# A hybrid decoder trunk on one core: one more feed-forward block by seven products, and ordinary work in pieces

## The chip, the cores and the metric

The kernel runs on one core of one Trainium2 chip. The metric is the device time of one execution in microseconds. A core has TensorE (PE, with its weight loads shown as PEld), VectorE (DVE), ScalarE (ACT), GpSimd (POOL) and SyncE (SP), each with an instruction queue of its own that is worked off in order. Matmuls write banks of PSUM; VectorE and ScalarE read them.

## The reference

Two layers work on 256 tokens of width 2048, all in float32:

```python
for l in range(DEPTH):                          # 2
    h = rms_norm(x, norm1_g[l])
    z = h @ w_in[l]                             # 2048 x 3584
    out_a = chunked_sgu(gelu(z[..., :2048]), ...)
    out_b = swa_sink_attention(...)             # window 128, 16 heads
    mixed = concat(rms_norm(out_a), rms_norm(out_b))
    x = x + mixed @ w_out[l]                    # 2048 x 2048
    h2 = rms_norm(x, norm2_g[l])
    x = x + (silu(h2 @ w_gate[l]) * (h2 @ w_up[l])) @ w_down[l]   # 2048 x 5632, back 5632 x 2048
```

The change lies in the last line, the feed-forward part.

## The kernel before, in words

Tokens lie in two tiles of 128. Weights arrive in chunks of 128 x 1024 numbers (512 KB): `raw_load` (L86) takes one of seven `raw` buffers in turn and issues the load on SP's queue. `split2` (L93) makes two parts of the chunk that together carry more of the float32 than one: ScalarE casts it to `wh` (L99), VectorE subtracts that from the chunk to give `wl` (L100). There are five buffers of each. `mm3` (L137) then multiplies activations and weights with three matmuls, high by high, high by low, low by high (L138 to L140), each 512 columns wide. The activations were transposed by TensorE beforehand and split in the same way.

The feed-forward width of 5632 is cut into 11 blocks of 512 columns. A block is done in one of two ways.

- *Ordinary* (`gate_up`, `even`, `unit`): 8 chunks of `w_gate` and 8 of `w_up`, each chunk with 12 matmuls over both token tiles, into two banks named `dacc`. ScalarE applies SiLU to the gate sums (L679), VectorE multiplies in the up sums (L683).
- *By seven products* (`seven`): gate and up for two token tiles form a 2 x 2 product of matrices, which a scheme of the Strassen kind does with seven products where the plain way has eight. Each chunk here (`s_unit`) serves one product with 6 matmuls. The activations' sums are made once per layer (`ext`). Per fourth of the inner width VectorE forms three sums of weight chunks (L613, L614, L619), and GpSimd's queue adds one more chunk into the tile `t2` with an accumulating load (L621). In the first phase five products go to five banks `m`; VectorE then combines them with five adds (L632 to L638). In the second phase the last two products go to two further banks `n`, which two adds (L651) bring in; SiLU and two multiplications (L652, L654) finish the block.

`S_BLOCKS` (L43) names the blocks that go by seven products: 3 to 10. Blocks 0 to 2 are ordinary. When a block is finished, `act_later` sets two calls of `act_T` (L573), two or three chunks later, each of which transposes 256 columns through one PSUM bank of the pool `pm` and splits them into a tile `aT` (L577, L578). The pool has ACTS = 6 of these.

`down` multiplies finished blocks by `w_down`. For each group of one or two blocks and each of four column ranges it runs 2 or 4 chunks of 12 matmuls into `dacc`, and VectorE adds the result to the residual `xres` (L704). Such work is ordinary as well: 12 matmuls for each split.

The two kinds of work are woven together when the program is recorded. A seven-product chunk gives VectorE more to do than TensorE, an ordinary chunk less. `debt` counts VectorE's assumed cost (VEC, VEC_P) less LOAD times TensorE's (MM); while it is positive, the loop takes chunks from `std_stream`:

```python
        other = std_stream()
        debt[0] = 0.0
        for _ in s_stream():
            while debt[0] > 0.0 and next(other, False):
                pass
```

`std_stream` follows `STD_ORDER` (L44) strictly: a `down` group whose transposed blocks are not there yet yields False, and nothing ordinary is taken in its place. What is left when the seven-product blocks are done runs at the end of the layer (the tail). On top of this the tile framework orders each engine's instructions when it records the program.

Of the kernel before, what the change touches and what calls it, by code (L numbers as in the profile page):

```python
# [21 lines left out]
P = 128  # L22
# [3 lines left out]
L = 2  # L26
# [13 lines left out]
NI = 3584 // NB  # L40
NFF = DFF // NB
ND = D // NB
S_BLOCKS = (3, 4, 5, 6, 7, 8, 9, 10)  # L43
STD_ORDER = (  # L44
    ("gu", 0), ("down", (0, 3)), ("gu", 1), ("down", (1, 4)), ("down", (5, 6)), ("gu", 2),
    ("down", (2, 7)), ("down", (8, 9)), ("down", (10,)),
)
ACTS = 6
VEC = 1.14
VEC_P = 0.6  # L50
MM = 0.227
LOAD = 0.91
RL = 512
WARM = 12

# [12 lines left out]
def trunk(ctx, tc, x, xt, w_in, w_out, w_gate, w_up, w_down, sgu_w, sgu_g, consts,  # L68
# [39 lines left out]

    def vec(n, cost=VEC):
        debt[0] += n * cost  # L110
# [7 lines left out]
    def later(delay, fn):  # L118
        pending.append((clock[0] + delay, next(serial), fn))
# [14 lines left out]
        pool, tag = ((pm, "sm"), (pd, "dacc"), (pa, "acc"), (pd, "dacc"))[next(turns) % 4]  # L134
        return pool.tile(shape, F32, tag=tag, name=name)

    def mm3(acc, ah, al, wh, wl, first, last):  # L137
        nc.tensor.matmul(acc, ah, wh, start=first, stop=False)  # L138
        nc.tensor.matmul(acc, ah, wl, start=False, stop=False)  # L139
        nc.tensor.matmul(acc, al, wh, start=False, stop=last)  # L140

    def unit(src, acts, acc, first, last):
        raw = raw_load(src, 2 if clock[0] < 4 else 1)
# [131 lines left out]
    for lay in range(L):  # L275
# [297 lines left out]
        def act_T(b, c, sg, pairs_f=pairs_f):  # L573
            ps = pm.tile([P, 2, SEQ], F32, tag="sm", name="ps_f")
            transpose_pair([sg[t][:, 2 * c * P : (2 * c + 2) * P] for t in range(NTOK)], ps)
            pair = pair_tile("aT")
            nc.scalar.copy(pair[:, 0], ps)  # L577
            nc.vector.tensor_tensor(pair[:, 1], ps, f(pair[:, 0]), ALU.subtract)  # L578
            vec(1, VEC_P)
            pe(2)  # L580
            pairs_f.setdefault(b, []).append(pair)

        def act_later(b, sg, act_T=act_T):
            for c in range(2):
                later(2 + c, lambda c=c: act_T(b, c, sg))

        def seven(b, lay=lay, pairs2=pairs2, ext2=ext2, act_later=act_later):
            bank = [pa.tile([P, NB], F32, tag="acc", name=f"m{i}") for i in range(5)]

            def s_unit(raw, m, i, op, first, last):  # L590
                wh, wl = split2(raw)
                for j in range(2):
                    ah, al = (op(2 * i + j, h) for h in range(2))
                    mm3(bank[m], ah, al, wh[:, j, :], wl[:, j, :], first and j == 0, last and j == 1)
                pe(6)
                tick(0.5)

            def a_op(k, t):
                return lambda p, h: pairs2[p][:, h, k, t * P : (t + 1) * P]

            def e_op(n):
                return lambda p, h: ext2[p][:, h, n, :]

            kept = []
            for i in range(4):
                b11 = raw_load(w_gate[lay, b, i, 0])
                b12 = raw_load(w_up[lay, b, i, 0])
                b22 = raw_load(w_up[lay, b, i, 1])
                t2 = ap.tile([P, 2, NB], F32, tag="spt", name="t2", bufs=4)
                first, last = i == 0, i == 3  # L610
                s_unit(b11, 0, i, a_op(0, 0), first, last)
                yield
                nc.vector.tensor_tensor(b11, b11, b12, ALU.add)  # L613
                nc.vector.tensor_tensor(t2, b11, b22, ALU.add)  # L614
                s_unit(b11, 1, i, e_op(1), first, last)
                vec(1)
                vec(1)
                yield
                nc.vector.tensor_tensor(b12, b12, b22, ALU.add)  # L619
                s_unit(t2, 3, i, e_op(2), first, last)  # L620
                nc.gpsimd.dma_start(t2, w_gate[lay, b, i, 1], accum_op=ALU.add)  # L621
                vec(1)
                yield
                s_unit(b12, 2, i, e_op(0), first, last)
                yield
                s_unit(b22, 4, i, e_op(3), first, last)
                yield
                kept.append(t2)
            m1 = zp.tile([P, NB], F32, tag="z", name="m1")
            nc.scalar.copy(m1, bank[0])  # L630
            u1 = zp.tile([P, NB], F32, tag="z", name="u1")
            nc.vector.tensor_tensor(u1, bank[3], m1, ALU.add)  # L632
            c22 = zp.tile([P, NB], F32, tag="z", name="c22")
            c21 = zp.tile([P, NB], F32, tag="z", name="c21")
            nc.vector.tensor_tensor(c21, bank[2], u1, ALU.add)
            nc.vector.tensor_tensor(c22, bank[1], c21, ALU.add)
            nc.vector.tensor_tensor(u1, bank[1], u1, ALU.add)
            nc.vector.tensor_tensor(u1, bank[4], u1, ALU.add)  # L638
            vec(5, VEC_P)
            yield  # L640
            bank = [pa.tile([P, NB], F32, tag="acc", name=f"n{i}") for i in range(2)]
            for i in range(4):
                b21 = raw_load(w_gate[lay, b, i, 1])
                first, last = i == 0, i == 3
                s_unit(b21, 0, i, a_op(1, 0), first, last)
                yield
                s_unit(kept[i], 1, i, a_op(1, 1), first, last)
                yield
            sg = [m1, c21]
            for t, m in ((0, m1), (1, c21)):  # L650
                nc.vector.tensor_tensor(m, bank[t], m, ALU.add)  # L651
                nc.scalar.activation(m, m, AF.Silu, scale=rstd2[t])  # L652
            for t, c in ((0, u1), (1, c22)):
                nc.vector.scalar_tensor_tensor(sg[t], c, nrstd2[t], sg[t], ALU.mult, ALU.mult)  # L654
            vec(4, VEC_P)
            act_later(b, sg)
            yield

        seven_done = [False]

        def s_stream(seven=seven):
            for b in S_BLOCKS:
                yield from seven(b)
# [7 lines left out]
                    yield True  # L671
            return acc

        def gate_up(b, even=even, act_later=act_later):
            acc = yield from even(b, w_gate)
            sg = []
            for t in range(NTOK):
                s = zp.tile([P, NB], F32, tag="z", name="sg")
                nc.scalar.activation(s, acc[t], AF.Silu, scale=rstd2[t])  # L679
                sg.append(s)  # L680
            acc = yield from even(b, w_up)
            for t in range(NTOK):
                nc.vector.scalar_tensor_tensor(  # L683
                    sg[t], acc[t], rstd2[t], sg[t], ALU.mult, ALU.mult
                )
            vec(NTOK, VEC_P)
            act_later(b, sg)

        def down(blocks, final, lay=lay, pairs_f=pairs_f, norm_block=norm_block, ss1=ss1, pairs1=pairs1):
            for n in range(ND):  # L690
                while any(len(pairs_f.get(b, [])) < 2 for b in blocks):
                    yield False
                acc = new_acc() if seven_done[0] else new_acc(pd, "dacc")
                for k, b in enumerate(blocks):
                    for c in range(2):
                        pair = pairs_f[b][c]
                        unit(
                            w_down[lay, b, n, c], [(pair, 0), (pair, 1)], acc,
                            k == 0 and c == 0, k == len(blocks) - 1 and c == 1,
                        )  # L700
                        yield True
                for t in range(NTOK):
                    xs = xres[:, t, n * NB : (n + 1) * NB]
                    nc.vector.tensor_tensor(xs, acc[t], xs, ALU.add)  # L704
                    vec(1, VEC_P)
                    if final and lay == L - 1:
                        nc.sync.dma_start(out[t * P : (t + 1) * P, n * NB : (n + 1) * NB], xs)
                if final and lay < L - 1:
                    norm_block(n, ss1, pairs1, lay + 1, C_G1)

        def std_stream(gate_up=gate_up, down=down):
            for k, (kind, what) in enumerate(STD_ORDER):
                if kind == "gu":
                    yield from gate_up(what)
                else:
                    yield from down(what, k == len(STD_ORDER) - 1)

        other = std_stream()
        debt[0] = 0.0
        for _ in s_stream():  # L720
            while debt[0] > 0.0 and next(other, False):
                pass
        seven_done[0] = True
        for went in other:
# [90 lines left out]
```

## Time and profile before

| | |
|---|---|
| three runs | 1959.99, 1961.52, 1965.34 us; median 1961.52 us |
| profiled execution | 1963.79 us, span 1962.1 us, granted clock 1.000 |
| PE busy, wide matmuls | 1947.1 us (99%); 8942 matmul instructions |
| VectorE busy | 1660.7 us (85%) |
| ScalarE busy | 1131.1 us (58%) |
| GpSimd busy | 120.3 us (6%) |
| HBM read | 416.47 MB, 214 GB/s over the span with the writes |
| feed-forward part, layer 0 and layer 1 | first `m` matmul at 288.3 and 1264.4 us |

The span runs from the first to the last instruction; the device time has 1.7 us more around it. Busy shares are means over stages: in the attention part VectorE is busy for 31 to 42 of 50 us, in the feed-forward part for 43 to 49. A matmul's row has a modelled end and overlaps the next row, so TensorE's pace is read from the starts.

### The profile page before, as it was taken

How to read it: one execution, taken by the hardware profiler on the slowest of the kernel's cores; microseconds unless marked ns; L12 is line 12 of the kernel's file. 1: busy time of each engine (PE TensorE's matmuls, PEld its weight loads, DVE VectorE, ACT ScalarE, POOL GpSimd, SP SyncE). 2: the span in 40 equal slices, each digit the busy share in tenths (PEclk: the TensorE clock that was granted, in tenths of full speed). 3: DMA queues.
4: the chain of work that ended last, by engine and by line, in shares of the span. 5: the costliest groups of instructions: out<-in, count | busy, mean ns of one | idle time of the engine just before them, and what ended most of it. 6: DMA issues, size and time to landing. Idle time of an engine off the chain costs nothing.

```text
span 1962.1 us, 24613 instructions
## 1 busy us (share of the span) xinstructions
PE 1947.1 (99%) x8942; PEld 1596.4 (81%) x8942; DVE 1660.7 (85%) x1883; ACT 1131.1 (58%) x1429; POOL 120.3 (6%) x129
## 2 busy tenths in 40 slices
PE   9999999999999999999999999999999999999999
PEld 7788888878878888888888888888888788888887
DVE  6776689989989899999667866899899898999984
ACT  7465566655655556656455565666556565565562
POOL 1210000000000000000002100000000000000000
PEclk9999999999999999999999999999999999999999
DMA  8854558677686776867655455676776767767773
GB/s 319 270 167 154 189 165 245 202 235 215 219 257 207 230 239 198 255 220 244 195 187 192 158 162 183 185 232 195 234 234 222 242 213 226 238 216 253 217 244 108
DMA packets 118554, 420.22 MB, mean 214 GB/s; under 512 B 13040, under 2 KB 15216, under 8 KB 118432
## 3 DMA queue, kind: packets, MB, share of 16 engines
q1 hardware_dynamic: 106928, 377.57, 55.7%
q0 software_dynamic: 11360, 41.00, 11.8%
q8 instruction: 70, 1.15, 0.2%
q14 instruction: 52, 0.43, 0.1%
q10 hardware_dynamic: 144, 0.08, 0.0%
HBM read 416.47 MB, written 4.23 MB: 214 GB/s over the span
## 4 chain that ended last, share of the span: by engine, by line
PE 88%; DVE 7%; DMA 3%; issue 2%; ACT 1%; POOL 0%; SPq 0%; ACTq 0%; DVEq 0%
PE dacc L138 10%; PE dacc L139 10%; PE dacc L140 10%; PE acc L138 9%; PE acc L140 9%; PE acc L139 9%; PE m L140 6%; PE m L139 6%; PE m L138 6%; DVE wl L100 3%; PE n L140 3%; PE n L139 3%; PE n L138 3%; PE ps_v L399 1%; DMA raw<-in_w_in_dram 1%
## 5 line engine op out<-in xcount | busy, mean ns | idle before, releaser
L99 ACT CAST wh<-raw 128x1024 fp32r<-128x1024 f32 (+1 forms) x770 | 794.1, 1049 | 657.4 <-PE acc L140 162.9
L100 DVE TENSOR_TENSOR wl<-raw,wh 128x1024 fp32r<-128x1024 f32 (+1 forms) x770 | 920.2, 1218 | 193.3 <-ACT wh L99 184.7
L138 PE MATMUL dacc<-wh,aT 128*128 128x512 f32 x576 | 225.2, 393 | 4.1 <-DVE xres L704 3.6
L139 PE MATMUL dacc<-wl,aT 128*128 128x512 f32 x576 | 225.0, 391 | 0.0
L140 PE MATMUL dacc<-wh,aT 128*128 128x512 f32 x576 | 224.8, 390 | 0.0
L139 PE MATMUL m<-wl,ext 128*128 128x512 f32 x512 | 200.6, 392 | 1.2 <-DVE wl L100 1.1
L138 PE MATMUL m<-wh,ext 128*128 128x512 f32 x512 | 200.1, 391 | 0.4 <-ACT wh L99 0.4
L140 PE MATMUL m<-wh,ext 128*128 128x512 f32 x512 | 199.4, 389 | 0.0
L138 PE MATMUL acc<-wh,hT 128*128 128x512 f32 x448 | 180.3, 404 | 0.2 <-ACT wh L99 0.2
L139 PE MATMUL acc<-wl,hT 128*128 128x512 f32 x448 | 175.4, 391 | 0.8 <-DVE wl L100 0.8
L140 PE MATMUL acc<-wh,hT 128*128 128x512 f32 x448 | 175.3, 391 | 0.0
L99 ACT CAST wh<-t 128x1024 fp32r<-128x1024 f32 x128 | 134.7, 1053 | 49.3 <-PE dacc L140 26.3
L100 DVE TENSOR_TENSOR wl<-t,wh 128x1024 fp32r<-128x1024 f32 x128 | 155.8, 1217 | 8.2 <-ACT wh L99 5.3
L138 PE MATMUL dacc<-wh,hT 128*128 128x512 f32 x384 | 151.1, 394 | 1.4 <-ACT sg L679 1.1
L138 PE MATMUL acc<-wh,aT 128*128 128x512 f32 x384 | 151.3, 394 | 0.0
L140 PE MATMUL acc<-wh,aT 128*128 128x512 f32 x384 | 149.8, 390 | 0.0
L139 PE MATMUL dacc<-wl,hT 128*128 128x512 f32 x384 | 149.7, 390 | 0.0
L140 PE MATMUL dacc<-wh,hT 128*128 128x512 f32 x384 | 149.7, 390 | 0.0
L139 PE MATMUL acc<-wl,aT 128*128 128x512 f32 x384 | 149.7, 390 | 0.0
L621 POOL DMA_DIRECT2D t<-in_w_gate_dram x64 | 54.7, 854 | 1337.8 <-DVE wl L100 769.7
L138 PEld LDWEIGHTS dacc<-wh,aT 128*128 128x128 f32 x576 | 107.7, 188 | 29.5 <-DVE xres L704 6.2
L139 PEld LDWEIGHTS dacc<-wl,aT 128*128 128x128 f32 x576 | 108.2, 188 | 22.9 <-DVE wl L100 0.8
(150 smaller groups left out, 2973.4 us busy)
## 6 DMA issues: line engine op xcount, KB each, us to landing
raw<-in_w_gate_dram SPq DMA_DIRECT2D x176, 512.0 KB, 5.5
raw<-in_w_up_dram SPq DMA_DIRECT2D x176, 512.0 KB, 4.5
raw<-in_w_down_dram SPq DMA_DIRECT2D x176, 512.0 KB, 4.6
raw<-in_w_in_dram SPq DMA_DIRECT2D x108, 512.0 KB, 4.5
raw<-in_w_out_dram SPq DMA_DIRECT2D x64, 512.0 KB, 3.3
t<-in_w_gate_dram POOLq DMA_DIRECT2D x64, 512.0 KB, 7.2
bias<-rdram POOLq DMA_DIRECT2D x8, 512.0 KB, 5.4
raw<-in_w_in_dram SPq DMA_DIRECT2D x8, 256.0 KB, 5.6
```

Source lines behind the costliest of these rows:

```text
L99: nc.scalar.copy(wh[:, j : j + step, :], src)
L100: nc.vector.tensor_tensor(wl[:, j : j + step, :], src, f(wh[:, j : j + step, :]), ALU.subtract)
L138: nc.tensor.matmul(acc, ah, wh, start=first, stop=False)
L139: nc.tensor.matmul(acc, ah, wl, start=False, stop=False)
L140: nc.tensor.matmul(acc, al, wh, start=False, stop=last)
L399: nc.tensor.matmul(pv[:, i, :], pt[:, i * nkb + b, :], zkv[b][:, (NKV + g) * HD : (NKV + g + 1) * HD], start=b == 0, stop=b == nkb - 1,)
L621: nc.gpsimd.dma_start(t2, w_gate[lay, b, i, 1], accum_op=ALU.add)
```

## The change

Block 2 goes by seven products too, nine blocks instead of eight. Ordinary work is cut into pieces: the gate half of a block, its up half, and each column range of a `down` group. At the end of each piece the first piece in `STD_ORDER` whose inputs are there is taken. A finished block's transposes are held (`held`) until a tile `aT` is left for them after what earlier groups still need (`room`, `admit`); after a first phase, ordinary work is taken also while more than HOLD = 2 are held. LOAD goes from 0.91 to 0.95. In `seven` the second phase adds onto bank 0 and bank 2 of the first phase, in which the other results already stand, with no fresh banks, and each sum tile's chunk comes one place later. The combination has four adds, the second phase one, and SiLU reads bank 0 in PSUM.

```diff
-S_BLOCKS = (3, 4, 5, 6, 7, 8, 9, 10)
+S_BLOCKS = (2, 3, 4, 5, 6, 7, 8, 9, 10)
 STD_ORDER = (
-    ("gu", 0), ("down", (0, 3)), ("gu", 1), ("down", (1, 4)), ("down", (5, 6)), ("gu", 2),
-    ("down", (2, 7)), ("down", (8, 9)), ("down", (10,)),
+    ("gu", 0), ("down", (0, 2)), ("down", (3, 4)), ("gu", 1), ("down", (1, 5)), ("down", (6, 7)), ("down", (8, 9)), ("down", (10,)),
 )
 ACTS = 6
+HOLD = 2
-LOAD = 0.91
+LOAD = 0.95
...
+        def room(b, made=made, freed=freed):
+            at = next(i for i, c in enumerate(chunks) if b in c)
+            missing = sum(2 - made.count(x) for c in chunks[:at] for x in c)
+            return len(made) - freed[0] + missing < ACTS
+
+        def admit(act_T=act_T, held=held, made=made, room=room):
+            for e in list(held):
+                if room(e[0]):
+                    held.remove(e)
+                    made.append(e[0])
+                    act_T(*e)
+
+        def act_later(b, sg, held=held, admit=admit):
+            def come(c):
+                held.append((b, c, sg))
+                admit()
+
             for c in range(2):
-                later(2 + c, lambda c=c: act_T(b, c, sg))
+                later(2 + c, lambda c=c: come(c))
...
-            bank = [pa.tile([P, NB], F32, tag="acc", name=f"m{i}") for i in range(5)]
+            bank = {}
...
+                if m not in bank:
+                    bank[m] = pa.tile([P, NB], F32, tag="acc", name=f"m{m}")
...
             nc.vector.tensor_tensor(u1, bank[3], m1, ALU.add)
+            c12 = zp.tile([P, NB], F32, tag="z", name="c12")
             c22 = zp.tile([P, NB], F32, tag="z", name="c22")
-            c21 = zp.tile([P, NB], F32, tag="z", name="c21")
-            nc.vector.tensor_tensor(c21, bank[2], u1, ALU.add)
-            nc.vector.tensor_tensor(c22, bank[1], c21, ALU.add)
-            nc.vector.tensor_tensor(u1, bank[1], u1, ALU.add)
-            nc.vector.tensor_tensor(u1, bank[4], u1, ALU.add)
-            vec(5, VEC_P)
+            nc.vector.tensor_tensor(c12, bank[1], u1, ALU.add)
+            nc.vector.tensor_tensor(c22, bank[2], c12, ALU.add)
+            nc.vector.tensor_tensor(c12, bank[4], c12, ALU.add)
+            vec(4, VEC_P)
             yield
-            bank = [pa.tile([P, NB], F32, tag="acc", name=f"n{i}") for i in range(2)]
-            for i in range(4):
-                b21 = raw_load(w_gate[lay, b, i, 1])
-                first, last = i == 0, i == 3
-                s_unit(b21, 0, i, a_op(1, 0), first, last)
-                yield
-                s_unit(kept[i], 1, i, a_op(1, 1), first, last)
-                yield
-            sg = [m1, c21]
-            for t, m in ((0, m1), (1, c21)):
-                nc.vector.tensor_tensor(m, bank[t], m, ALU.add)
-                nc.scalar.activation(m, m, AF.Silu, scale=rstd2[t])
+            for i in range(5):
+                if i < 4:
+                    b21 = raw_load(w_gate[lay, b, i, 1])
+                    s_unit(b21, 0, i, a_op(1, 0), False, i == 3, skip_group_check=True)
+                    yield
+                if i > 0:
+                    s_unit(kept[i - 1], 2, i - 1, a_op(1, 1), False, i == 4, skip_group_check=True)
+                    yield
+            sg = [m1, u1]
+            nc.vector.tensor_tensor(u1, bank[2], u1, ALU.add)
+            for t, src in ((0, bank[0]), (1, u1)):
+                nc.scalar.activation(sg[t], src, AF.Silu, scale=rstd2[t])
...
+            pieces = []
+            for kind, what in STD_ORDER:
+                if kind == "gu":
+                    sg = []
+                    pieces += [((), half, (what, True, sg)), ((), half, (what, False, sg))]
+                else:
+                    last = what == chunks[-1]
+                    pieces += [(what, down, (what, n, last)) for n in range(ND)]
+            begun = set()
+            while pieces:
+                for k, (need, fn, args) in enumerate(pieces):
+                    if any(len(pairs_f.get(b, [])) < 2 for b in need):
+                        continue
...
+                pieces.pop(k)
...
+                yield from fn(*args)
...
-        for _ in s_stream():
-            while debt[0] > 0.0 and next(other, False):
+        for full in s_stream():
+            while (debt[0] > 0.0 or full and len(held) > HOLD) and next(other, False):
                 pass
```

More of the change, by code (lines that the diff above doesn't have):

```diff
@@ L135, in small_ps, with mm3 @@
         return pool.tile(shape, F32, tag=tag, name=name)
[L137 to L140, printed above, removed]
+    def mm3(acc, ah, al, wh, wl, first, last, **more):
+        nc.tensor.matmul(acc, ah, wh, start=first, stop=False, **more)
+        nc.tensor.matmul(acc, ah, wl, start=False, stop=False, **more)
+        nc.tensor.matmul(acc, al, wh, start=False, stop=last, **more)
     def unit(src, acts, acc, first, last):
@@ L581, in act_T, with s_unit @@
             pairs_f.setdefault(b, []).append(pair)
-        def act_later(b, sg, act_T=act_T):
+        held = []
+        made = []
+        freed = [0]
+        chunks = [what for kind, what in STD_ORDER if kind == "down"]
+        def room(b, made=made, freed=freed):
[12 more added lines that the diff above has]
+                admit()
             for c in range(2):
-                later(2 + c, lambda c=c: act_T(b, c, sg))
+                later(2 + c, lambda c=c: come(c))
         def seven(b, lay=lay, pairs2=pairs2, ext2=ext2, act_later=act_later):
-            bank = [pa.tile([P, NB], F32, tag="acc", name=f"m{i}") for i in range(5)]
-            def s_unit(raw, m, i, op, first, last):
+            bank = {}
+            def s_unit(raw, m, i, op, first, last, **more):
                 wh, wl = split2(raw)
+                if m not in bank:
+                    bank[m] = pa.tile([P, NB], F32, tag="acc", name=f"m{m}")
                 for j in range(2):
                     ah, al = (op(2 * i + j, h) for h in range(2))
-                    mm3(bank[m], ah, al, wh[:, j, :], wl[:, j, :], first and j == 0, last and j == 1)
+                    mm3(bank[m], ah, al, wh[:, j, :], wl[:, j, :], first and j == 0, last and j == 1, **more)
                 pe(6)
@@ L626, in seven @@
                 s_unit(b22, 4, i, e_op(3), first, last)
-                yield
                 kept.append(t2)
+                yield last
             m1 = zp.tile([P, NB], F32, tag="z", name="m1")
@@ L632, in seven @@
             nc.vector.tensor_tensor(u1, bank[3], m1, ALU.add)
+            c12 = zp.tile([P, NB], F32, tag="z", name="c12")
             c22 = zp.tile([P, NB], F32, tag="z", name="c22")
-            c21 = zp.tile([P, NB], F32, tag="z", name="c21")
-            nc.vector.tensor_tensor(c21, bank[2], u1, ALU.add)
-            nc.vector.tensor_tensor(c22, bank[1], c21, ALU.add)
-            nc.vector.tensor_tensor(u1, bank[1], u1, ALU.add)
-            nc.vector.tensor_tensor(u1, bank[4], u1, ALU.add)
-            vec(5, VEC_P)
-            yield
-            bank = [pa.tile([P, NB], F32, tag="acc", name=f"n{i}") for i in range(2)]
-            for i in range(4):
-                b21 = raw_load(w_gate[lay, b, i, 1])
-                first, last = i == 0, i == 3
-                s_unit(b21, 0, i, a_op(1, 0), first, last)
-                yield
-                s_unit(kept[i], 1, i, a_op(1, 1), first, last)
-                yield
-            sg = [m1, c21]
-            for t, m in ((0, m1), (1, c21)):
-                nc.vector.tensor_tensor(m, bank[t], m, ALU.add)
-                nc.scalar.activation(m, m, AF.Silu, scale=rstd2[t])
-            for t, c in ((0, u1), (1, c22)):
+            nc.vector.tensor_tensor(c12, bank[1], u1, ALU.add)
+            nc.vector.tensor_tensor(c22, bank[2], c12, ALU.add)
+            nc.vector.tensor_tensor(c12, bank[4], c12, ALU.add)
+            vec(4, VEC_P)
+            yield
+            for i in range(5):
[10 more added lines that the diff above has]
+                nc.scalar.activation(sg[t], src, AF.Silu, scale=rstd2[t])
+            vec(1, VEC_P)
+            for t, c in ((0, c12), (1, c22)):
                 nc.vector.scalar_tensor_tensor(sg[t], c, nrstd2[t], sg[t], ALU.mult, ALU.mult)
-            vec(4, VEC_P)
+            vec(2, VEC_P)
             act_later(b, sg)
@@ L672, in even, with half @@
             return acc
-        def gate_up(b, even=even, act_later=act_later):
-            acc = yield from even(b, w_gate)
-            sg = []
+        def half(b, gate, sg, even=even, act_later=act_later):
+            acc = yield from even(b, w_gate if gate else w_up)
             for t in range(NTOK):
[L678 to L681, printed above, removed]
-            for t in range(NTOK):
[L683 to L687, printed above, removed]
@@ L689, in down @@
-        def down(blocks, final, lay=lay, pairs_f=pairs_f, norm_block=norm_block, ss1=ss1, pairs1=pairs1):
-            for n in range(ND):
-                while any(len(pairs_f.get(b, [])) < 2 for b in blocks):
-                    yield False
[L693 to L716, printed above, removed]
+                if gate:
+                    s = zp.tile([P, NB], F32, tag="z", name="sg")
+                    nc.scalar.activation(s, acc[t], AF.Silu, scale=rstd2[t])
+                    sg.append(s)
+                else:
+                    nc.vector.scalar_tensor_tensor(
+                        sg[t], acc[t], rstd2[t], sg[t], ALU.mult, ALU.mult
+                    )
@@ new lines, in half, with down @@
+            if not gate:
+                vec(NTOK, VEC_P)
+                act_later(b, sg)
+        def down(blocks, n, final, lay=lay, pairs_f=pairs_f, norm_block=norm_block, ss1=ss1,
+                 pairs1=pairs1, freed=freed, admit=admit):
+            acc = new_acc() if seven_done[0] else new_acc(pd, "dacc")
+            for k, b in enumerate(blocks):
+                for c in range(2):
+                    pair = pairs_f[b][c]
+                    unit(
+                        w_down[lay, b, n, c], [(pair, 0), (pair, 1)], acc,
+                        k == 0 and c == 0, k == len(blocks) - 1 and c == 1,
+                    )
+                    yield True
+            for t in range(NTOK):
+                xs = xres[:, t, n * NB : (n + 1) * NB]
+                nc.vector.tensor_tensor(xs, acc[t], xs, ALU.add)
+                vec(1, VEC_P)
+                if final and lay == L - 1:
+                    nc.sync.dma_start(out[t * P : (t + 1) * P, n * NB : (n + 1) * NB], xs)
+            if final and lay < L - 1:
+                norm_block(n, ss1, pairs1, lay + 1, C_G1)
+            if n == ND - 1:
+                freed[0] += 2 * len(blocks)
+                admit()
@@ new lines, in std_stream @@
+        def std_stream(half=half, down=down, pairs_f=pairs_f):
+            pieces = []
[3 more added lines that the diff above has]
+                    pieces += [((), half, (what, True, sg)), ((), half, (what, False, sg))]
+                else:
+                    last = what == chunks[-1]
[5 more added lines that the diff above has]
+                        continue
+                    if fn is half and not args[1] and args[0] not in begun:
+                        continue
+                    if fn is half and args[1] and begun:
+                        continue
+                    break
+                else:
+                    yield False
+                    continue
+                pieces.pop(k)
+                if fn is half:
+                    (begun.add if args[1] else begun.discard)(args[0])
+                yield from fn(*args)
```

## The prediction, made before the changed kernel was run

> **What bounds the kernel now.** I read the page's busy line, then the timeline of TensorE, the groups by form, the timelines of VectorE and ScalarE, the table of windows and the chain. All durations are from the one profiled execution, 1963.79 us with a span of 1962.1 us; the median of the three runs shown is 1961.52 us, 2.3 us lower, and the forecast is given against that median. About 0.3% (5.9 us) is what a measurement of this kernel can tell from no change.
>
> ```profile
> PE 1947.1 (99%) x8942; PEld 1596.4 (81%) x8942; DVE 1660.7 (85%) x1883; ACT 1131.1 (58%) x1429; POOL 120.3 (6%) x129
> ```
>
> A matmul's 0.39 us is modelled and overlaps the next, so 99% alone proves little. The starts in the timeline of PE tell more:
>
> ```profile
> 579.04 0.39 PE L140 MATMUL dacc<-wh,aT 128*128 128x512 f32 x1
> 579.27 0.39 PE L138 MATMUL m<-wh,ext 128*128 128x512 f32 x1
> 579.50 0.39 PE L139 MATMUL m<-wl,ext 128*128 128x512 f32 x1
> 581.37 0.50 PE L138 MATMUL dacc<-wh,aT 128*128 128x512 f32 x1 [1.49 <-DVE xres L704]
> ```
>
> Starts stand 0.227 us apart; the last row stands 1.87 us after the one before, a loss of 1.65 us. Adding up all such excesses over 0.227 between wide matmuls, the feed-forward stretch of layer 0 (first product matmul at 288.3 us, tail ending about 955) loses 9.1 us and that of layer 1 (1264.4 to 1957.2) 7.6 us. Of these, 5.2 and 3.8 us are in gaps that lose over 0.15 us; the rest are some 39 losses of 0.1 us per layer. So TensorE binds, and at most about 9 us of real waiting could be won back.
>
> VectorE is the next engine. Groups by form:
>
> ```profile
> L100 DVE TENSOR_TENSOR wl<-raw,wh 128x1024 fp32r<-128x1024 f32 x766 | 917.5, 1220 | 192.0 <-ACT wh L99 183.4
> ...
> L613 DVE TENSOR_TENSOR raw<-raw 128x1024 f32<-128x1024 f32 x64 | 78.2, 1222 | 1.6
> ...
> L651 DVE TENSOR_TENSOR m<-n,m 128x512 f32<-128x512 f32 x16 | 10.9, 682 | 0.0
> ```
>
> These too overlap when queued. The timeline of DVE, then that of ACT:
>
> ```profile
> 392.70 4.62 DVE L100 TENSOR_TENSOR wl<-raw,wh 128x1024 fp32r<-128x1024 f32 x4
> 401.35 3.50 DVE L100 TENSOR_TENSOR wl<-raw,wh 128x1024 fp32r<-128x1024 f32 x3 [4.03 <-ACT wh L99]
> ```
>
> ```profile
> 400.27 3.89 ACT L99 CAST wh<-raw 128x1024 fp32r<-128x1024 f32 x4 [6.38 <-PE dacc L140]
> ```
>
> Four subtractions in 4.62 us are 1.135 us apart; the narrow PSUM ones start 0.60 us apart (median of their back-to-back starts). Where VectorE idles here it waits for ScalarE's cast, which waits for TensorE to free one of five weight buffers: back-pressure. The table of windows, in the same stretch of layer 1:
>
> ```profile
> 1650.00:1700.00 50.00, 50.00 (x226) 41.40 (x225) 48.50 (x48) 30.79 (x33) 1.70 (x2) 1.00 0.68 204
> 1700.00:1750.00 50.00, 50.00 (x222) 40.98 (x221) 43.88 (x43) 30.19 (x32) 1.70 (x2) 1.00 0.66 213
> 1750.00:1800.00 50.00, 50.00 (x226) 41.38 (x225) 48.67 (x47) 31.27 (x33) 3.41 (x4) 1.00 0.87 262
> ```
>
> Columns: stretch, PE, PEld, DVE, ACT, POOL, clock, DMA share, GB/s. The clock is 1.00. VectorE ran at 97% for 50 us at a time with no PE time lost. From 296 to 900 us it is busy 556.9 of 604 us, 92.2%.
>
> **The change, part by part.** *Block 2 by seven products.* An ordinary block takes 192 wide matmuls (16 weight chunks of 12), a seven-product block 168. One block in each of two layers: 48 fewer, in both recorded instruction orders 8076 against 8028 (12 are warm-up). 48 x 0.227 = 10.9 us off TensorE. Transposes are as many as before.
>
> On VectorE each such block takes 28 splits in place of 16 and 12 sums of weights: 24 wide instructions more. Its combining of products is 7 narrow ones in place of 2.
>
> *Second-phase products onto used banks.* L651's two adds go in every seven-product block: one add into bank 2 stays, one is not needed, and the first combination is one shorter. That is two narrow VectorE instructions fewer in each of the eight old blocks of a layer. Over the program the two orders differ by +48 wide and -22 narrow: 48 x 1.135 - 22 x 0.60 = +41.3 us, 20.6 us a layer.
>
> ScalarE gains 24 casts of 1.05 us and two copies of 0.58 us; at 58% busy that is hidden, and if it were not, it would cost 26 us at most. SiLU of the first half now reads PSUM; the nearest row, L679, takes 684 ns from PSUM against 724 ns for L652 from SBUF: nothing. Eight more accumulating loads go through POOL's queue, 0.85 us of issue each, on an engine at 6%; their data wait for the second phase, one chunk later in it than before, so they cost nothing unless that lead goes (up to 7.2 us each, their median time to landing on the page). Loads on SP's queue stay at 704.
>
> *Does VectorE still fit?* Without the tail (16 ordinary chunks in both versions, light on VectorE), the stretch of 604 us needs 604 - 5.4 = 598.6 us of TensorE, and VectorE 556.9 + 20.6 = 577.5 us: 96.5%. Break-even is 577.5 / 604 = 95.6%: VectorE must hold more than that, or the saving is gone. The 97% windows above hold it. Against the orders I added up VectorE's work less TensorE's up to each weight chunk. In the old order this backlog climbs by 6.6, 5.7, 5.6 and 4.9 us in places; in the new one by 6.2 us just after the start, then never by more than 4.0. Five buffered chunks hold at least 5 x 1.36 = 6.8 us of matmuls, less about 2.2 for cast and subtraction. So although the average is tighter, the order is smoother. I take 0 to 3 us of new lateness a layer, 1.5 likeliest, because in the new order several seven-product chunks are torn apart by ordinary ones in one place of the layer, a sign that they were judged late.
>
> *Ordinary work in pieces, held transposes.* These add no instructions; they choose the order. What they could win back is in the chain:
>
> ```profile
> 568.71 6.74 DMA raw<-in_w_down_dram
> ...
> 576.62 2.36 DVE wl L100 x2
> ...
> 580.63 0.69 DVE xres L704
> ```
>
> A down chunk landed late, VectorE stood still for 2.85 us, its subtractions came late, and behind them in its queue the two adds that free the dacc banks: the 1.65 us of the PE row above. SP issues a load when the buffer seven loads earlier is free. In the old order VectorE reaches two weight chunks per layer 2.27 us of its own work before their buffers could even be released; in the new one the least distance is +3.4 us, and loads with less than 5 us fall from 106 to 28. Pieces that begin under 1.5 us of PE work after the previous one left its banks fall from five a layer to three. The gaps at the two DMA places sum to 5.6 us over both layers; I count half, 3 us, as won.
>
> A held transpose leaves its two SBUF tiles occupied longer; nothing queues behind it on TensorE, since it is not yet in the queue. When two are admitted at once the second needs the only bank of that pool, free after 0.58 + 0.60 us; the order puts 7 or more matmuls (1.6 us) between any two: 0 to 1 us.
>
> The Trainium skill (Trace Analysis, Matmuls) says that independent matmul groups should rotate through different PSUM banks so that evacuation overlaps the next group; the second phase now does the reverse. In the order, bank 2's first second-phase matmul stands 4.1 to 12.7 us of TensorE work behind its last first-phase one, and two adds of 0.60 us have to fit between. The trace of before shows no such wait, since its second phase has banks of its own (n); the nearest is a piece waiting for its dacc adds, 1.49 us in the PE row above. I price the wait at 0; its upper end is a rival.
>
> Sum: -10.9 + 3 (lateness, both layers) - 3 (late loads) = -10.9 us. 1963.79 goes to 1952.9; from the median, **1950.6 us**.
>
> **The rivals.**
> 1. *VectorE becomes the bound; slower.* For: 96.5% needed, no stretch of before held this for over 50 us. Against: its idle time is back-pressure, and backlog climbs are smaller. It decides at 95.6%. If it holds 94%, a layer's stretch lasts 577.5 / 0.94 = 614.4 us, +10.4 each, 1982 us; at 95%, 607.9, +3.9 each, 1969 us.
> 2. *VectorE was the bound all along.* Matmul busy time misleads and PEld is 81% against 85% for VectorE. Then all 41.3 us are paid: 2003 us. Against: starts 0.227 us apart and idle VectorE. The Trainium skill (Trace Analysis, Identifying the Most-Contended Engine) gives this rule: judge TensorE by weight loading, VectorE by occupancy. By it this time would come; the rows disagree.
> 3. *Bank reuse waits.* If VectorE is late by a queued subtraction, 1 us in each of 18 blocks: +18 against -10.9, 1969 us; at half, 1960 us.
> 4. *The saving is there, but lateness eats a part*: 3 us a layer without anything won back, 1957 us.
> 5. *All waits over 0.15 us go* as well: 1961.5 - 10.9 - 9 = 1942 us.
>
> **How the numbers follow.** Forecast with its own spread (1946 to 1955): 0.58. Rival 5 or near it: 0.09. Rival 4: 0.12. Rival 1: 0.13. Rival 2: 0.02. Rival 3: 0.06. Under 1955.6 lie the first two and a little of rival 4: faster 0.69. Same (1955.6 to 1967.4): most of rival 4, half of rival 3 and the mild end of rival 1, 0.15. Slower: the rest of rivals 1 and 3, rival 2, and the bad end of rival 4, 0.16. The range of 1944 to 1970 leaves out the ends of rivals 1, 2 and 5.
>
> **What would show it.** Right: starts still 0.227 us apart; VectorE at 48 of 50 us in windows from 300 to 900 us; the tail beginning 5 us earlier in each layer; no w_down load in the chain of the first layer; wait of `wh` for PE buffers smaller. Wrong: PE rows waiting for `wl` (L100) or `xres` beyond 10 us in sum; windows with DVE near 50 and fewer than 220 matmuls; first matmul of a second phase waiting for the add that reads bank 2.

## The result, and the profile after

| | before | changed |
|---|---|---|
| median, us | 1960.76 (1959.78 to 1965.34, 4 runs) | 1944.58 (1944.02 to 1945.16, 4 runs) |
| ratio | | 0.9915, 95% interval 0.9899 to 0.993 |
| profiled execution, us | 1963.79, span 1962.1 | 1945.16, span 1943.5 |

The changed kernel is faster by 16.2 us, where 10.9 were forecast. The two profiled executions, which the traces below come from, lie 18.6 us apart. The page's busy line of the changed kernel:

```profile
PE 1933.4 (99%) x8894; PEld 1588.5 (82%) x8894; DVE 1699.4 (87%) x1909; ACT 1151.3 (59%) x1455; POOL 127.1 (7%) x137
```

TensorE has 48 matmul rows fewer; VectorE is busy 38.7 us longer. The shares of the chain, first of before, then of the changed kernel, show where the rest went:

```profile
PE 88%; DVE 7%; DMA 3%; issue 2%; ACT 1%; POOL 0%; SPq 0%; ACTq 0%; DVEq 0%
```

```profile
PE 94%; DVE 3%; issue 1%; ACT 1%; DMA 1%; SPq 0%; ACTq 0%; DVEq 0%
```

VectorE does more work and yet stands less often on the path. The list of waits bears on the reason. Columns: who waited for whom, us in total, times, longest. Two rows of before:

```profile
ACT wh L99 <- PE dacc L140: 177.5, 108, 6.4
...
ACT wh L99 <- DMA raw<-in_w_down_dram: 13.3, 4, 5.2
```

The same in the changed kernel:

```profile
ACT wh L99 <- PE dacc L140: 105.9, 71, 3.0
...
ACT wh L99 <- DMA raw<-in_w_in_dram: 8.3, 10, 4.7
```

The four casts that waited for a late down chunk wait no longer (the `w_in` loads belong to the attention part), and ScalarE's wait for the weight buffers of ordinary work is shorter, its longest piece half as long. In return casts wait longer for the sums of weights that VectorE forms: 264.0 us for the two sums that overwrite `raw`, where it was 197.6. That idle time of ScalarE costs nothing as long as TensorE has work in store. What TensorE itself waits for fell too. Of its list before:

```profile
PE dacc L138 <- DVE xres L704: 3.8, 4, 1.5
...
PE m L139 <- DVE wl L100: 1.1, 3, 0.6
```

In the changed kernel's list only these rows are left of matmuls into `dacc` and `m`:

```profile
PE dacc L138 <- ACT wh L99: 0.5, 2, 0.3
...
PE m L138 <- ACT wh L99: 0.3, 2, 0.2
```

The table of windows, stretches in layer 0 of the changed kernel (PE, PEld, DVE, ACT, POOL, clock, DMA share, GB/s):

```profile
350.00:400.00 50.00, 50.00 (x226) 41.41 (x225) 49.83 (x47) 30.82 (x33) 3.39 (x4) 1.00 0.74 230
...
650.00:700.00 50.00, 50.00 (x226) 41.35 (x226) 49.75 (x47) 32.71 (x35) 2.56 (x3) 1.00 0.84 271
```

VectorE is full for 50 us, and TensorE still begins 226 matmuls, as many as in the fullest windows that the prediction shows of before. From 300 to 900 us VectorE is busy 92.2% before and 96.6% in the changed kernel:

```profile
300.00:900.00 600.00, 595.87 (x2651) 489.08 (x2650) 553.46 (x536) 352.78 (x370) 25.55 (x30) 1.00 0.73 226
```

```profile
300.00:900.00 600.00, 599.32 (x2671) 493.04 (x2670) 579.89 (x557) 367.61 (x388) 29.81 (x35) 1.00 0.73 233
```

The distances between starts of neighbouring wide matmuls, each less 0.227 us, are added up here from the first product to the last matmul of the feed-forward part. This excess is 5.4 us in layer 0 and 4.7 in layer 1; in the kernel before it is 9.6 and 7.9 (the prediction, which ended its sum in layer 0 before the tail was over, has 9.1 and 7.6). That is 7.4 us won, 6.6 of them in losses of more than 0.15 us each, and the longest single loss is 0.43 us where it was 1.65. With the 10.9 us of the matmuls saved this makes 18.3 of the 18.6 us between the two profiled executions.

### The profile page after: what moved, and what is told of

Same layout as the page of the kernel before. It is cut to its first block, busy times and chain, and to the rows that moved or that the text cites. A ratio compares the mean times of both kernels' runs of the same rounds, so it can differ in the third digit from the quotient of the medians.

```text
span 1943.5 us, 24615 instructions
## 1 busy us (share of the span) xinstructions
PE 1933.4 (99%) x8894; PEld 1588.5 (82%) x8894; DVE 1699.4 (87%) x1909; ACT 1151.3 (59%) x1455; POOL 127.1 (7%) x137
## 3 DMA queue, kind: packets, MB, share of 16 engines
q0 software_dynamic: 12512, 45.19, 12.5%
## 4 chain that ended last, share of the span: by engine, by line
PE 94%; DVE 3%; issue 1%; ACT 1%; DMA 1%; SPq 0%; ACTq 0%; DVEq 0%
PE m L140 11%; PE m L139 11%; PE m L138 11%; PE acc L138 10%; PE acc L140 10%; PE acc L139 10%; PE dacc L138 9%; PE dacc L139 9%; PE dacc L140 9%; DVE wl L100 2%; PE ps_v L399 1%; PE ps_f L208 1%; ACT wh L99 1%; PE ps_s L357 1%; PE ps_t L208 1%
## 5 line engine op out<-in xcount | busy, mean ns | idle before, releaser
L138 PE MATMUL m<-wh,ext 128*128 128x512 f32 x576 | 225.7, 392 | 0.0
L139 PE MATMUL m<-wl,ext 128*128 128x512 f32 x576 | 224.6, 390 | 0.0
L140 PE MATMUL m<-wh,ext 128*128 128x512 f32 x576 | 224.3, 389 | 0.0
L100 DVE TENSOR_TENSOR wl<-t,wh 128x1024 fp32r<-128x1024 f32 x144 | 175.2, 1219 | 21.8 <-ACT wh L99 18.1
L99 ACT CAST wh<-t 128x1024 fp32r<-128x1024 f32 x144 | 151.4, 1052 | 57.5 <-PE dacc L140 40.0
L138 PE MATMUL m<-wh,hT 128*128 128x512 f32 x432 | 168.5, 390 | 0.3 <-ACT wh L99 0.3
L140 PE MATMUL m<-wh,hT 128*128 128x512 f32 x432 | 168.1, 389 | 0.0
L139 PE MATMUL m<-wl,hT 128*128 128x512 f32 x432 | 168.1, 389 | 0.0
L644 POOL DMA_DIRECT2D t<-in_w_gate_dram x72 | 61.5, 854 | 1327.3 <-DVE wl L100 828.5
```

What stands on the lines that cost most here:

```text
L99: nc.scalar.copy(wh[:, j : j + step, :], src)
L100: nc.vector.tensor_tensor(wl[:, j : j + step, :], src, f(wh[:, j : j + step, :]), ALU.subtract)
L138: nc.tensor.matmul(acc, ah, wh, start=first, stop=False, **more)
L139: nc.tensor.matmul(acc, ah, wl, start=False, stop=False, **more)
L140: nc.tensor.matmul(acc, al, wh, start=False, stop=last, **more)
```

## The experiments

Every time below is a median beside the kernel before on the same chip, where that one took 1961.5, 1963.1 and 1962.9 us in the three groups of runs.

**Block 2 alone.** The kernel before with

```diff
-S_BLOCKS = (3, 4, 5, 6, 7, 8, 9, 10)
+S_BLOCKS = (2, 3, 4, 5, 6, 7, 8, 9, 10)
-    ("gu", 0), ("down", (0, 3)), ("gu", 1), ...
+    ("gu", 0), ("down", (0, 2)), ("down", (3, 4)), ("gu", 1), ...
```

> The kernel before with block 2 by seven products and the new list of ordinary work, but taken strictly in turn, transposes not held, second phase on fresh banks, LOAD 0.91. Theory A (the order decides what waits remain): the same 10.9 us of matmuls go, but in its recorded order VectorE's work climbs over TensorE's by 14.1, 11.3 and 25.0 us in three places of a layer, because no ordinary work is ready there. Less the some 5 us that five buffered chunks cover, that is some 35 us lost in each layer: about 1961 - 11 + 70 = 2020 us (1990 to 2035). Theory B (only the amounts of work on the engines count, and VectorE's share in the woven stretch, 95.4% by the orders, is no more than in the changed kernel): 1945 to 1955 us.

Measured: 2074.4 us, ratio 1.0573 (1.0557 to 1.059). Theory B is refuted; theory A has the direction and not the size. Windows of this kernel:

```profile
501.00:505.00 4.00, 4.00 (x20) 3.30 (x19) 4.00 (x5) 0.73 (x1) 0.00 (x0) 1.00 0.51 178
505.00:509.00 4.00, 2.14 (x9) 0.97 (x7) 4.00 (x5) 3.07 (x4) 0.00 (x0) 1.00 0.00 0
509.00:513.00 4.00, 3.51 (x10) 2.25 (x10) 4.00 (x5) 2.87 (x4) 0.85 (x1) 0.61 0.40 131
```

VectorE is busy without a break while TensorE is idle for half of four microseconds: no ordinary chunk is ready, and seven-product chunks alone need more of VectorE than of TensorE. Excess starts sum to 56.4 and 57.3 us in the two layers, 96 us more than before. Another 17.4 us are waits of transposes for the end of a block (`ps_f` for L653 in its list), which the count of climbs did not hold. 96 + 17 - 11 = 102 of the 109 us between the two profiled executions; the rest was not located. Late loads have a part in it that was not parted off: casts wait 60.4 us for down chunks, 33 times. The third row shows one more cost, told at the end.

**The order and the used banks, without block 2.** The changed kernel with

```diff
-S_BLOCKS = (2, 3, 4, 5, 6, 7, 8, 9, 10)
+S_BLOCKS = (3, 4, 5, 6, 7, 8, 9, 10)
-LOAD = 0.95
+LOAD = 0.91
```

and the old list of ordinary work.

> The changed kernel with eight blocks by seven products again (3 to 10), the old list of ordinary work and LOAD 0.91; pieces taken when ready, held transposes and the second phase on used banks stay. The matmuls are as many as before. Theory A: with the pieces no backlog climbs over 5.8 us and no chunk is needed before its buffer can be released, so the waits over 0.07 us in the feed-forward part fall from 16.7 us to about 10 as in the changed kernel: 1954 to 1957 us. Theory B: TensorE's work is that of before, VectorE had room: 1960 to 1962 us.

Measured: 1955.9 us, ratio 0.997 (0.9959 to 0.9982); excess starts are 5.7 and 5.2 us, and casts wait 0.2 us for down chunks where it was 13.3. So the order together with the used banks is worth 5.6 us without a matmul saved. The two are not parted here: the used banks also take 32 narrow adds off VectorE, whose busy time falls by 16.9 us. At the 0.07 us per us found below, that work would by itself be worth little over 1 us, by estimate. From here to the changed kernel (1945.2 us, run again below on another chip) it is 10.7 us as the times stand and 12 by the ratios; the 48 matmuls are 10.9.

**Strict turns.** In the changed kernel pieces are taken as the list has them:

```diff
-                for k, (need, fn, args) in enumerate(pieces):
-                    if any(len(pairs_f.get(b, [])) < 2 for b in need):
-                        continue
...
-                else:
+                k, (need, fn, args) = 0, pieces[0]
+                if any(len(pairs_f.get(b, [])) < 2 for b in need):
                     yield False
                     continue
```

> The changed kernel with its ordinary pieces taken strictly in the order of the list; all else stays. Its recorded order has as many matmuls and sums; two chunks a layer are needed 5.7 us before their buffer can be released and one climb reaches 5.4 us. Theory A: 1 to 4 us a layer for the late load, 1946 to 1952 us. Rival (taking pieces when ready does nothing, the rest of the change does): 1943 to 1946 us.

Measured: 1951.0 us, ratio 0.9945 (0.993 to 0.996). Casts wait 8.8 us for two down chunks again, and in the timeline of PE the loss of layer 0 follows:

```profile
519.43 0.39 PE L138 MATMUL m<-wh,ext 128*128 128x512 f32 x1
521.12 0.50 PE L139 MATMUL m<-wl,ext 128*128 128x512 f32 x1 [1.30 <-DVE wl L100]
```

This is one place in each layer; the whole difference to the changed kernel is 5.8 us, some 2.9 us a layer.

**Six load buffers.** `bufs=7` of `raw` becomes 6.

> The changed kernel with six load buffers (raw) in place of seven. The recorded order of work is nearly the same, but a load can start one chunk later: loads with less than 5 us of VectorE's work between the release of the buffer and the first use go from 28 to 92, the least from 3.4 to 2.3 us. Theory A (late loads are what the old order lost time by): landing takes 4.5 to 6.3 us, so VectorE stands still more often and has little to make it up: 1947 to 1955 us. Rival (loads are hidden in any order): 1943 to 1946 us.

Measured: 1950.8 us (1948.7 to 1954.7), ratio 0.9945 (0.993 to 0.996), within theory A. Its list of waits has loads again:

```profile
ACT wh L99 <- DMA raw<-in_w_gate_dram: 16.7, 14, 2.6
ACT wh L99 <- DMA raw<-in_w_down_dram: 14.9, 18, 2.3
```

The work and its order are nearly the same, and loads begin one chunk later: later loads alone cost about 5.6 us here.

**Fresh banks.** In the changed kernel

```diff
-                    s_unit(b21, 0, i, a_op(1, 0), False, i == 3, skip_group_check=True)
+                    s_unit(b21, 5, i, a_op(1, 0), i == 0, i == 3)
-                    s_unit(kept[i - 1], 2, i - 1, a_op(1, 1), False, i == 4, skip_group_check=True)
+                    s_unit(kept[i - 1], 6, i - 1, a_op(1, 1), i == 1, i == 4)
```

with the five adds and the two of L651 as before.

> The changed kernel with the second phase on two fresh banks and the old combination: 36 narrow VectorE instructions more, 21.6 us of VectorE's time. Theory A: in its order VectorE's backlog climbs by 7.5 and 7.3 us in two places of a layer and two chunks are needed up to 10 us before their buffers are free; 5 to 10 us a layer come back: 1955 to 1965 us. Theory B (by amounts): VectorE's share in the stretch stays 95.7%, nothing is lost: 1944 to 1947 us. A gain over the changed kernel would mean that the used banks cost waits.

Measured: 1969.1 us, ratio 1.0036 (1.0023 to 1.0049), 4 us past theory A's range. Excess starts are 12.9 and 11.6 us, and two down chunks in layer 0 stand in its chain with 5.9 and 6.0 us. The 21.6 us of VectorE change the mix and thus the order, so this does not part the banks from the order; it does show that fresh banks with their adds are no gain in sum, and that in this order the ninth block does not pay with them. One more thing can be read from it. On every engine it has as many instructions as the kernel with block 2 alone (8894 on PE, 1945 on VectorE, 1455 on ScalarE, 137 on GpSimd), and it was timed in the same group of runs: 1969.1 against 2074.4 us. The order in which the same work stands is worth 105 us.

**No holding.** `come` calls `act_T` at once.

> The changed kernel without holding transposes: each is issued two or three chunks after its block. The recorded order has the same largest climb (6.2 us) and least distance of loads (3.4 us). Theory A: same time within 2 us, 1943 to 1947 us, as the holding only guards the buffers. Rival: holding is what removed the waits; then 1950 us or more.

Measured: 1942.4 us, ratio 0.99 (0.9885 to 0.9915): better than expected, so both were run again, five rounds each.

> The changed kernel again, to stand beside the one without holding on one chip: 1944 to 1946 us.

Measured: 1945.2 us (1945.05 to 1945.5), ratio 0.9911 (0.9896 to 0.9926).

> The changed kernel without holding transposes again. If the 2 us between the two are real, 1942 to 1943 us and an interval that lies below that of the changed kernel or nearly so; if they are the spread between chips, the two medians agree within 1 us.

Measured: 1942.4 us (1942.37 to 1942.46), ratio 0.9897 (0.9882 to 0.9911). The intervals against before overlap, the runs themselves do not: holding costs 2.8 us, and this is the fastest version that computes the whole function. About 1 us of it lies in each layer's seven-product stretch, over half of that in the wide matmuls that follow transposes (from the last transpose to the next wide start 1.2 us a layer in sum with holding, 0.6 without); 0.8 us was not located. Holding is not the part that removed the waits.

**More and less work for VectorE.** One line in the changed kernel, which forms a part of the second sum a second time, over 256 or 512 columns:

```diff
                 nc.vector.tensor_tensor(t2, b11, b22, ALU.add)
+                nc.vector.tensor_tensor(t2[:, 0, :256], b11[:, 0, :256], b22[:, 0, :256], ALU.add)
```

> The changed kernel in which VectorE computes a quarter of the first weight sum a second time for each fourth of a block's inner width: 72 instructions of 256 columns more, about 0.33 us each, 24 us of VectorE's time over the program; the result stays. Nothing else changes. Theory A (VectorE still has room, only local backlogs count): its share in the stretch goes to 97.8% by the orders, the largest climb to 7.0 us at the start and 4.4 later: 1944 to 1948 us. Rival (VectorE binds already in the changed kernel): all 24 us are paid, 1968 us; in between, say 1955 us, it sits at the edge.

> As the kernel with a quarter of the sum done twice, but half of it: 72 instructions of 512 columns more, 0.60 us each, 43 us of VectorE's time. Theory A: its share in the stretch comes to 99.0% by the orders and near 100% with the dependent sums 0.12 us further apart; the edge is passed a little: 1948 to 1958 us. Rival (VectorE binds in the changed kernel): 1988 us.

Measured: 1954.2 us, ratio 0.9958 (0.9941 to 0.9974), and 1967.5 us, ratio 1.0024 (1.0014 to 1.0034). Theory A was too kind: 9 of 24 us and 22 of 43 us are paid. Then the other way, with the third sum formed over half of its columns only (it leaves out the other half, so the kernel's result is not the function's):

```diff
-                nc.vector.tensor_tensor(b12, b12, b22, ALU.add)
+                nc.vector.tensor_tensor(b12[:, 0], b12[:, 0], b22[:, 0], ALU.add)
```

> The changed kernel in which the third sum of weight chunks (b12 + b22) is formed over half its columns only, so that product uses wrong numbers in the other half: 72 instructions of 512 columns in place of 1024, 38 us less for VectorE, its share in the stretch 92.5% by the orders, the rest of the order much the same. Theory A': VectorE is just not the bound in the changed kernel (its waits over 0.07 us sum to 10 us, most of them short and in fixed places): 1941 to 1944 us. Rival (the changed kernel still pays for VectorE as the two kernels with more of it did, about 0.4 to 0.5 us per us): 1925 to 1930 us.

Measured: 1942.5 us, ratio 0.9898 (0.9881 to 0.9914). Taking some 38 us off wins 2.7. In this kernel casts still wait 12.5 us for loads of the feed-forward weights, and its time is that of the fastest one: such a wait need not cost time. The windows from 300 to 900 us, with 38 us less, with 24 and with 43 us more (the changed kernel's stands above):

```profile
300.00:900.00 600.00, 599.83 (x2676) 493.95 (x2675) 564.46 (x557) 369.95 (x387) 29.82 (x35) 1.00 0.76 234
```

```profile
300.00:900.00 600.00, 596.29 (x2646) 487.18 (x2645) 584.45 (x585) 363.66 (x382) 28.99 (x34) 1.00 0.74 230
```

```profile
300.00:900.00 600.00, 594.51 (x2623) 482.26 (x2622) 587.34 (x579) 360.85 (x379) 28.99 (x34) 1.00 0.73 229
```

DVE goes from 94.1% over 96.6% to 97.4% and 97.9%; matmuls begun fall from 2676 over 2671 to 2646 and 2623. The price of a microsecond of VectorE rises from 0.07 below the changed kernel's point to 0.4 just above it. It stands at the edge. Whether the same work at other places would have the same price was not tested.

**LOAD 0.97** in place of 0.95, same instructions.

> The changed kernel with LOAD 0.97 in place of 0.95: the same instructions, but the seven-product blocks come denser and the tail is longer; VectorE's share in the stretch is 97.7% by the orders, climbs reach 6.5, 6.1 and 5.4 us. Theory A' (the share inside the stretch and the climbs count): as in the kernel with 24 us more, 1949 to 1956 us. Rival (the amount of work over the program counts): 1944 to 1946 us.

Measured: 1953.9 us, ratio 0.9955 (0.9941 to 0.997), 8.7 us more than the changed kernel with the same instructions. The share inside the woven stretch (97.2% busy from 300 to 900 us) and the order count, not the amount over the program; slack in the tail does not help. Share and order were not parted here.

## Why the prediction was right, and where it was off

- *Matmuls saved, 10.9 us*: right. The trace has 48 rows fewer at 0.227 us, and the kernel without block 2 lies 10.7 us (12 by the ratios) above the changed one.
- *VectorE fits at 96.5%*: right; 96.6% measured from 300 to 900 us, 96.1% from the first product to the last. So was rival 1's doubt, one step further on: 24 us more eat 9 us, over half of the gain. Its break-even of 95.6% was plain arithmetic of busy time and said nothing of how lateness grows. Rival 2 would have charged the full VectorE work; VectorE is busy 38.7 us longer and the kernel 16.2 us faster, and the price is 0.07 us per us on one side of the changed kernel. The Trainium skill (Perfetto Trace Analysis, Identifying the Most-Contended Engine) judges TensorE by weight loading beside the share of peak arithmetic, and VectorE by occupancy. By weight loading VectorE, at 87%, would come before PEld, at 82%; the measured times say that here TensorE binds nearly throughout.
- *Lateness, 3 us lost in both layers*: right in size as far as one kernel can tell; the one with 38 us less of VectorE wins 2.7.
- *Late loads, 3 us won*: the mis-sized term. 16.2 - 10.9 is a net gain of 5.3 us, so if 2.7 were lost again, some 8 us were won. The starts say much the same: losses of more than 0.15 us fell from 9.0 us in both layers to 2.4. I counted half of the 5.6 us at the two places, and nothing for the pauses at the ends of pieces and the other losses, although the count of pieces that follow closely upon each other had fallen from five to three. How the 6.6 us part between loads and ends of pieces was not measured. The order with the used banks shows 5.6 us net by itself. Three other numbers were wrong on the way. Loads with less than 5 us are about 50 in the old order when counted again, not 106 (28 in the new one is right). The tail of layer 0 ends at 984.6 us, not at about 955. And the tail is not 16 chunks in both: from the last product to the end of layer 1 it is 55.4 us before and 47.3 after, 20 and 17 chunks. Three more ordinary chunks thus lay in the stretch, and VectorE's share in it was a little lower than I charged.
- *Used banks, 0*: right. No row of the changed kernel has a product matmul waiting for the adds that read its bank; the only wait of `m` in its list is 0.3 us for `wh`. The Trainium skill (Perfetto Trace Analysis, Matmuls) advises independent groups of matmuls to rotate through banks, so that the reading of one overlaps the next. Here other matmuls give that overlap, since in the order 4.1 us or more of them lie between.
- *Held transposes, 0 to 1 us*: too low; 2.8 us.
- Signs named ahead: starts at 0.227 us, VectorE at 48 of 50 us and no down load in layer 0's chain came; the tail began 1.9 us earlier in layer 0, not 5, since three chunks of it had moved into the stretch. Casts wait 318 us for matmuls to free a weight buffer, where it was 403, as named.

The forecast's own spread began at 1946 us, so the result lay between it and rival 5 (all longer waits gone, 1942 us), inside the range. Rival 5 was nearer to what happened than its chance of 0.09 says: 6.6 of its 9 us came.

## What to carry to other kernels

When two engines are both over 90% busy, add up their work in the recorded order, not only in sum: with the same instructions, two orders lay 105 us apart, by where other work stood ready. Count from the order, too, how far each load's buffer release lies before its next use. In the kernel before, the four loads needed before their buffer could be released (-2.27 us, two a layer) match in number the four casts that waited for down chunks. And probe how near the second engine is by giving it a little more and a little less to do: here the slope went from 0.07 to 0.4 within one step.

## What was not expected of the hardware

TensorE ran at half speed for some microseconds, at places where the kernel is far from idle. In the kernel with block 2 alone, TensorE waited three times between 1006 and 1011.5 us, for 2.13, 1.41 and 0.68 us, and had four transposes to do in between. The timeline of PE after that, and three windows of 3.4 us with their clock:

```profile
1012.41 0.63 PE L137 MATMUL acc<-wh,aT 128*128 128x512 f32 x1
1012.84 0.63 PE L138 MATMUL acc<-wl,aT 128*128 128x512 f32 x1
```

```profile
1008.30:1011.70 3.40, 1.04 (x5) 0.64 (x6) 3.40 (x5) 0.82 (x2) 0.00 (x0) 0.99 0.67 216
1011.70:1015.10 3.40, 3.40 (x9) 2.64 (x9) 1.40 (x2) 0.00 (x0) 0.00 (x0) 0.50 0.91 278
1015.10:1018.50 3.40, 3.40 (x19) 2.81 (x18) 0.69 (x1) 1.30 (x2) 0.00 (x0) 1.00 0.30 123
```

Starts stand 0.43 us apart in place of 0.227, at a granted clock of 0.50. The trace's record of the clock has eight such stretches before the program's last microseconds, seven of 3.41 us and one of 6.83, and they begin whole multiples of 3.41 us apart. In the 3.41 us before each of them TensorE was busy for 1.0 to 2.0 us by the profile, and the longest single pause shortly before was 1.3 to 2.3 us. The Trainium skill (TensorE: Matmul & The Clock Gate, What's actually happening) tells of such a gate: half of the clock pulses after an idle window of about 3.4 us. The trace agrees in the factor, 1.9, and in the 3.41 us; it differs in the condition, since no pause was that long and TensorE was not idle throughout any of these windows. How little work is little enough was not measured: the kernel before has one stretch of 3.41 us with 1.6 us of work, at 403 us, and kept its clock there. In the changed kernel, from 25 us until 8 us before its end, TensorE was busy for at least 2.5 of any 3.41 us, and the clock stayed at 1.00. The 30.7 us at half speed are worth some 15 us by estimate, a part of the excess starts above. So waits of TensorE can cost more than their own length when they come close together.
